# Low halves of the weights made by GpSimd in 256-column instructions instead of one instruction a tile

## Chip, cores and metric

The kernel runs on one core of a Trainium2 chip. The metric is the device time of one execution in microseconds (us); a run's time is the slowest core's, and there is one. Engines are named as the profile names them: PE is TensorE (PEld its weight loads), DVE is VectorE, ACT is ScalarE, POOL is GpSimd, SP is SyncE, which issues the DMAs.

## What is computed

The reference is a whole transformer block followed by a second block, on one sequence of 1024 tokens of width 1024, in float32. What matters here is that nearly all of it is matrix products of activations with weights:

```python
def first_block(x, ...):
        h = rmsnorm(x, norm_mix[l])
        proj = h @ w_in[l]
        y_a = retention(...) @ w_ret_o[l]
        y_b = nsa(...) @ w_nsa_o[l]
        merged = jax.nn.sigmoid(ga) * y_a + jax.nn.sigmoid(gb) * y_b
        x = x + merged @ w_out[l]
        x = x + conv_ffn(rmsnorm(x, norm_ffn[l]), w_up[l], conv_w[l], conv_b[l], w_down[l])
def second_block(x, c, ...):
        ada = c_act @ w_ada[l] + b_ada[l]
        proj = h @ w_in[l]
        mix = jnp.concatenate([y_rwkv, y_s5], axis=-1) @ w_out[l]
        ffn = (jax.nn.silu(h @ ffn_w_gate[l]) * (h @ ffn_w_up[l])) @ ffn_w_down[l]
```

`retention`, `nsa` (block-sparse attention), `rwkv7_time_mix` and `s5_mix` are sequence mixers between these products.

## The kernel before

**Products in split precision.** PE multiplies in the faster float32r format, so every operand is kept as two parts, a high part (rounded to float32r) and a low part (what the rounding left). A product of a weight tile and an activation is three sums: high x high, high x low, low x high. `mm3` (L216) issues them for one output tile of 128 x 512: first the 16 products with the weight's high part, then the 8 with its low part (for eight slices of 128 of the contraction, `kt` = 8). `mm3t` (L225) does it with weights as the moving operand.

**Loading a weight.** `wload` (L182) makes one tile of 128 output columns. SP loads the raw float32 weight into `wraw`, a tile of 128 partitions by up to eight slices of 128 columns (1024 columns; 512 or 640 where the contraction is shorter) at L197. ACT rounds it into `whi` (L199). POOL subtracts to make `wlo` (L200). `whi` and `wlo` have two buffers each, `wraw` two and, once there is room, a third that every third load goes to. So a buffer of `wlo` is free again when PE has done the low products of the tile before last, and a buffer of `wraw` when POOL has read it. `wload2` (L203) makes a pair of tiles side by side (`w2hi`, `w2lo`) with one subtraction for each of them at L213. `proj` (L234) calls `wload`, then `mm3` for one or two halves of the tokens, and evacuates each.

```python
        nc.scalar.activation(hi[:, :kt], raw[:, :kt], AF.Copy)
        nc.gpsimd.tensor_sub(lo[:, :kt], raw[:, :kt], hi[:, :kt].bitcast(F32))
```

**What else runs beside it.** DVE works on activations in SBUF: in the first feed-forward network `conv_gelu` (L1583) makes a convolution of width three from `at` into `ct` (L1596 to L1598), ACT applies the gelu (L1599), DVE multiplies by the second projection (L1616), ACT rounds to `ah` (L1617), and POOL makes `al` (L1618); `ah` and `al` are the operands of `down` (L1622). In `z_proj` (L1757) DVE makes the token shift in `ct` (L1772 to L1775). `s5_prep` (L995) builds tables of complex powers with long runs of DVE products of two SBUF tiles (L1072 to L1077), between the steps of that feed-forward network. `ada` (L1930) multiplies 96 weight tiles of 128 x 512 with a vector on DVE (L1943) beside the retention. `square_sum` (L255) adds squares at L263.

**What sets the order.** Each engine runs its instructions in a fixed order. It is chosen when the program is built, by a scheduler that goes by its own timing model, within the program's data dependencies and some extra edges (`side_by_side`, `hold`) that set the recurrent mixers and the feed-forward products side by side on PE. So a change of one instruction's size can move others. Dependencies are tracked by the region of a tile: a product waits for the writer of the slice that it reads.

Of the kernel before, what the change touches and what calls it, by code (L numbers as in the profile page):

```python
# [9 lines left out]
F32 = mybir.dt.float32  # L10
# [108 lines left out]
class Ctx:  # L119
# [62 lines left out]
    def wload(self, srcs, kt=KT, pool=None):  # L182

        nc = self.nc
        W = pool or self.W
        m = KT if pool is None else kt
        nb = 2 if pool is None else 1
        self.n_w += 1

        third = pool is None and self.WX is not None and self.n_w % 3 == 0  # L190
        raw = (self.WX if third else W).tile([128, m, 128], F32, name="wraw", bufs=1 if third else nb)
        hi = W.tile([128, m, 128], F32R, name="whi", bufs=nb)
        lo = W.tile([128, m, 128], F32R, name="wlo", bufs=nb)
        c = 0
        for src in srcs if isinstance(srcs, (list, tuple)) else [srcs]:
            n = src.shape[1]
            nc.sync.dma_start(raw[:, :kt, c:c + n], src.rearrange("(k p) n -> p k n", p=128))  # L197
            c += n
        nc.scalar.activation(hi[:, :kt], raw[:, :kt], AF.Copy)  # L199
        nc.gpsimd.tensor_sub(lo[:, :kt], raw[:, :kt], hi[:, :kt].bitcast(F32))  # L200
        return hi, lo

    def wload2(self, srcs, pool, kt=KT):  # L203

        nc = self.nc
        hi = pool.tile([128, kt, 256], F32R, name="w2hi")
        lo = pool.tile([128, kt, 256], F32R, name="w2lo")
        for e, src in enumerate(srcs):
            raw = self.W.tile([128, KT, 128], F32, name="wraw", bufs=2)
            nc.sync.dma_start(raw[:, :kt], src.rearrange("(k p) n -> p k n", p=128))  # L210
            sl = slice(e * 128, (e + 1) * 128)
            nc.scalar.activation(hi[:, :, sl], raw[:, :kt], AF.Copy)
            nc.gpsimd.tensor_sub(lo[:, :, sl], raw[:, :kt], hi[:, :, sl].bitcast(F32))  # L213
        return hi, lo

    def mm3(self, ps, w, a, t, kt=KT, late=False):  # L216
# [1797 lines left out]
```

## Time and profile before

| | |
|---|---|
| three runs | 3491.17 us median, 3486.78 to 3498.57 |
| the profiled execution | 3491.11 us, of which 3489.1 us are the span of its instructions |
| PE busy | 3350.0 us, 96% of the span |
| DVE busy | 1716.8 us, 49% |
| POOL busy | 1442.0 us, 41% |
| ACT busy | 1336.8 us, 38% |
| mean granted clock of PE | 0.982 of full speed |
| DMA | 371 MB, mean 106 GB/s |

An engine's busy time is the union of its instructions' spans, and an instruction that is held up while it runs counts as busy: a long mean duration can be work or a wait inside the instruction. Waits ahead of an instruction are idle time, put down to what ended them. PE's instructions overlap, and 48 products of 512 columns in a row take 48 equal steps, so the idle time of PE and the stretches at a lower clock are what can be gained there.

### The profile page before, as it was taken

What the parts mean: (1) busy time and instruction counts of PE and PEld (TensorE: products, weight loads), DVE (VectorE), ACT (ScalarE), POOL (GpSimd) and SP (SyncE); (2) the same over time, 40 slices, a digit from 0 to 9 for tenths busy, and PEclk for the clock granted to TensorE, in tenths of its full rate; (3) what the DMA queues carried; (4) which work ended last, traced back from release to release, by engine and by line L of the source; (5) the groups of instructions that cost most, each with busy time, mean ns of one, the idle gap of its engine ahead of it and who ended that gap; (6) DMA issues with size and microseconds to landing.
All of it is one profiled execution on the core that took longest, in us unless ns stands there. A gap on an engine that the chain in (4) does not pass through costs nothing. (4 is left out here: it accounts for less than half of the span.)

```text
span 3489.1 us, 49441 instructions
## 1 busy us (share of the span) xinstructions
PE 3350.0 (96%) x19080; PEld 2716.6 (78%) x19080; DVE 1716.8 (49%) x3313; ACT 1336.8 (38%) x2175; POOL 1442.0 (41%) x1081
## 2 busy tenths in 40 slices
PE   7999999998999998999989999999899999999998
PEld 6988788887788777887876777768777777778887
DVE  4456556555533774355674554564734344351112
ACT  4245346422334422243234444433353433342223
POOL 2333333210144444554554444325554443355544
PEclk9999999999999999999999999989999999999999
DMA  4211111455534434334533122234442221363332
GB/s 148 67 61 52 57 63 46 135 187 169 189 124 139 124 101 144 94 118 133 179 108 114 54 73 69 61 108 147 145 120 67 70 67 55 94 197 97 91 94 93
DMA packets 519813, 371.02 MB, mean 106 GB/s; under 512 B 31724, under 2 KB 455834, under 8 KB 518810
## 3 DMA queue, kind: packets, MB, share of 16 engines
q1 hardware_dynamic: 519578, 367.86, 34.3%
q8 instruction: 151, 2.47, 0.3%
q14 instruction: 84, 0.69, 0.1%
HBM read 313.44 MB, written 54.03 MB: 105 GB/s over the span
## 5 line engine op out<-in xcount | busy, mean ns | idle before, releaser
L200 POOL TENSOR_TENSOR wlo<-wraw,whi 128x1024 fp32r<-128x1024 f32 (+2 forms) x460 | 940.6, 2049 | 1290.7 <-PE mm L223 503.5
L199 ACT ACTIVATE whi<-wraw 128x1024 fp32r<-128x1024 f32 (+2 forms) x460 | 417.4, 909 | 703.7 <-PE mm L223 342.0
L223 PE MATMUL mm<-fh,whi 128*128 128x512 f32 x976 | 401.4, 413 | 10.0 <-ACT whi L199 4.9
L223 PE MATMUL mm<-fl,whi 128*128 128x512 f32 x976 | 393.2, 404 | 6.2 <-DVE fl L334 6.1
L223 PE MATMUL mm<-fh,wlo 128*128 128x512 f32 x976 | 270.2, 404 | 0.0
L223 PE MATMUL mm<-hh,whi 128*128 128x512 f32 x640 | 260.4, 407 | 5.4 <-DVE kc L252 3.7
L223 PE MATMUL mm<-hl,whi 128*128 128x512 f32 x640 | 260.9, 408 | 0.0
L223 PEld LDWEIGHTS mm<-fh,whi 128*128 128x128 f32 x976 | 185.9, 191 | 57.2 <-issue 6.5
L223 PEld LDWEIGHTS mm<-fl,whi 128*128 128x128 f32 x976 | 185.7, 191 | 47.0 <-DVE fl L334 9.3
L223 PE MATMUL b<-fh,whi 128*128 128x512 f32 x544 | 213.7, 393 | 1.2 <-ACT whi L199 0.7
L223 PE MATMUL b<-fl,whi 128*128 128x512 f32 x544 | 213.4, 392 | 0.0
L223 PEld LDWEIGHTS mm<-fh,wlo 128*128 128x128 f32 x976 | 179.0, 190 | 40.3 <-issue 3.6
L223 PE MATMUL mm<-ah,whi 128*128 128x512 f32 x429 | 177.1, 415 | 15.0 <-ACT ah L1617 9.3
L223 PE MATMUL mm<-hh,wlo 128*128 128x512 f32 x640 | 178.0, 400 | 0.0
L223 PE MATMUL mm<-al,whi 128*128 128x512 f32 x429 | 174.8, 408 | 0.0
L223 PEld LDWEIGHTS mm<-hh,whi 128*128 128x128 f32 x640 | 122.2, 191 | 27.9 <-issue 5.5
L223 PE MATMUL b<-fh,wlo 128*128 128x512 f32 x544 | 135.0, 390 | 6.3 <-POOL wlo L200 6.3
L223 PEld LDWEIGHTS mm<-hl,whi 128*128 128x128 f32 x640 | 122.1, 191 | 20.9
L223 PEld LDWEIGHTS mm<-hh,wlo 128*128 128x128 f32 x640 | 117.0, 189 | 21.5
L223 PE MATMUL mm<-ah,wlo 128*128 128x512 f32 x429 | 128.2, 407 | 0.3 <-POOL wlo L200 0.3
L588 ACT ACTIVATE s<-s,amn 128x640 f32<-128x640 f32 (+7 forms) x128 | 94.0, 735 | 80.3 <-DVE amn L584 74.3
L223 PEld LDWEIGHTS b<-fh,wlo 128*128 128x128 f32 x544 | 102.1, 188 | 28.3 <-POOL wlo L200 7.1
(601 smaller groups left out, 7117.5 us busy)
## 6 DMA issues: line engine op xcount, KB each, us to landing
wraw<-in_w_up SPq DMA_DIRECT2D x88, 512.0 KB
wraw<-in_w_in SPq DMA_DIRECT2D x84, 512.0 KB
ada_w<-in_w_ada SPq DMA_DIRECT2D x96, 256.0 KB
wraw<-in_ffn_w_gate SPq DMA_DIRECT2D x44, 512.0 KB
wraw<-in_ffn_w_up SPq DMA_DIRECT2D x44, 512.0 KB
wraw<-in_w_out SPq DMA_DIRECT2D x32, 512.0 KB
d_gab<-st SPq DMA_DIRECT2D x56, 256.0 KB
wraw<-in_w_down SPq DMA_DIRECT2D x48, 256.0 KB
```

Of the source, the lines that this page charges most:

```text
L199: nc.scalar.activation(hi[:, :kt], raw[:, :kt], AF.Copy)
L200: nc.gpsimd.tensor_sub(lo[:, :kt], raw[:, :kt], hi[:, :kt].bitcast(F32))
L223: self.nc.tensor.matmul(ps, w[x][:, k], a[y][k][:, t * 512:(t + 1) * 512], start=i == 0, stop=i == 3 * kt - 1)
L588: nc.scalar.activation(sb[r][:, :n], sb[r][:, :n], AF.Exp, bias=init, scale=-1.0, accum_out=st[:, 0, r:r + 1])
```

## The change

`wload` and `wload2` issue the subtraction for two slices (256 columns) at a time: four instructions for a tile of 1024 columns, two for 512, and for 640 two of 256 and one of 128. What is computed stays the same.

```diff
@@ wload
         nc.scalar.activation(hi[:, :kt], raw[:, :kt], AF.Copy)
-        nc.gpsimd.tensor_sub(lo[:, :kt], raw[:, :kt], hi[:, :kt].bitcast(F32))
+        for k in range(0, kt, 2):
+            sl = slice(k, min(k + 2, kt))
+            nc.gpsimd.tensor_sub(lo[:, sl], raw[:, sl], hi[:, sl].bitcast(F32))
         return hi, lo
@@ wload2
             nc.scalar.activation(hi[:, :, sl], raw[:, :kt], AF.Copy)
-            nc.gpsimd.tensor_sub(lo[:, :, sl], raw[:, :kt], hi[:, :, sl].bitcast(F32))
+            for k in range(0, kt, 2):
+                nc.gpsimd.tensor_sub(lo[:, k:k + 2, sl], raw[:, k:k + 2], hi[:, k:k + 2, sl].bitcast(F32))
```

Lines behind the first edit move by two, behind the second by three (L200 becomes L202, L223 becomes L226).

The change moves instructions. On PE, the low products of the first weight tile (`hh` is the activation's high part, `wlo` the weight's low part; Pool_49 is the semaphore that POOL raises) stood so before:

```order
L223 MATMUL mm<-hh_86,wlo 128x512 [waits Pool_49]
L223 MATMUL mm<-hh_87,wlo 128x512
L223 MATMUL mm<-hh_88,wlo 128x512
L223 MATMUL mm<-hh_89,wlo 128x512
L223 MATMUL mm<-hh_90,wlo 128x512
L223 MATMUL mm<-hh_91,wlo 128x512
L223 MATMUL mm<-hh_92,wlo 128x512
L223 MATMUL mm<-hh_93,wlo 128x512
```

and with the change:

```order
L226 MATMUL mm<-hh_86,wlo 128x512 [waits Pool_49]
L226 MATMUL mm<-hh_87,wlo 128x512
L226 MATMUL mm<-hh_88,wlo 128x512 [waits Pool_49]
L226 MATMUL mm<-hh_89,wlo 128x512
L226 MATMUL mm<-hh_90,wlo 128x512 [waits Pool_49]
L226 MATMUL mm<-hh_91,wlo 128x512
L226 MATMUL mm<-hh_92,wlo 128x512 [waits Pool_49]
L226 MATMUL mm<-hh_93,wlo 128x512
```

Each pair of products waits for its own piece; the pieces of a tile stand next to each other on POOL.

On PE in the first feed-forward network (its products at 1427 us of the trace of before; `b` and `mm` are the sums of two different weight tiles, `fh` and `fl` the activation), before:

```order
L223 MATMUL mm<-fh_9790,whi 128x512
L223 MATMUL mm<-fl_9798,whi 128x512
L223 MATMUL mm<-fh_9791,whi 128x512
L223 MATMUL mm<-fl_9799,whi 128x512
L223 MATMUL mm<-fh_9792,whi 128x512
L223 MATMUL mm<-fl_9800,whi 128x512
L223 MATMUL b_12781<-fh_9788,wlo 128x512
L223 MATMUL b_12781<-fh_9789,wlo 128x512
L223 MATMUL b_12781<-fh_9790,wlo 128x512
L223 MATMUL b_12781<-fh_9791,wlo 128x512
```

and with the change:

```order
L226 MATMUL mm<-fh_9965,whi 128x512
L226 MATMUL b_13132<-fh_9964,wlo 128x512
L226 MATMUL b_13132<-fh_9965,wlo 128x512
L226 MATMUL mm<-fl_9973,whi 128x512
L226 MATMUL b_13132<-fh_9966,wlo 128x512
L226 MATMUL b_13132<-fh_9967,wlo 128x512
L226 MATMUL mm<-fh_9966,whi 128x512
L226 MATMUL b_13132<-fh_9968,wlo 128x512
L226 MATMUL b_13132<-fh_9969,wlo 128x512
L226 MATMUL mm<-fl_9974,whi 128x512
```

The low products of the earlier tile moved ahead of high products of the later one, a pair at a time. Such a place occurs a few times; about one PE instruction in eleven has another place in the order than before, most of them in the attention and the retention, where two streams of products stand side by side.

## Rows read from the trace of the kernel before

**Rows 1.** The page's first part: busy time, share of the span, instructions.
```profile
span 3489.1 us, 49441 instructions
...
PE 3350.0 (96%) x19080; PEld 2716.6 (78%) x19080; DVE 1716.8 (49%) x3313; ACT 1336.8 (38%) x2175; POOL 1442.0 (41%) x1081
```

**Rows 2.** PE's waits: for whom, us in total, times, longest.
```profile
PE mm L223 <- ACT ah L1617: 9.3, 1, 9.3
...
PE b L223 <- POOL wlo L200: 6.3, 2, 3.4
...
PE mm L231 <- DVE ct L1616: 4.3, 1, 4.3
```

**Rows 3.** Busy time in four stretches: PE, PEld, DVE, ACT, POOL; then granted clock, DMA.
```profile
650.00:900.00 250.00, 229.09 (x1404) 203.27 (x1403) 142.76 (x275) 66.42 (x107) 34.06 (x14) 0.98 0.54 168
1100.00:1350.00 250.00, 231.03 (x1145) 190.01 (x1144) 164.00 (x367) 84.51 (x123) 110.54 (x73) 0.97 0.42 126
1550.00:1800.00 250.00, 230.46 (x1157) 195.83 (x1156) 165.35 (x179) 80.05 (x114) 131.39 (x102) 0.95 0.47 147
...
2400.00:2600.00 200.00, 188.56 (x944) 159.25 (x942) 104.31 (x115) 76.45 (x104) 104.69 (x67) 0.96 0.41 126
```

**Rows 4.** POOL's groups by shape: busy us, mean ns, idle before and its releasers.
```profile
L200 POOL TENSOR_TENSOR wlo<-wraw,whi 128x1024 fp32r<-128x1024 f32 x284 | 689.2, 2429 | 882.6 <-PE mm L223 351.6 <-ACT whi L199 270.5 <-issue 94.7
L200 POOL TENSOR_TENSOR wlo<-wraw,whi 128x512 fp32r<-128x512 f32 x112 | 146.4, 1313 | 289.2 <-PE mm L223 125.7 <-ACT whi L199 83.9 <-PE b L223 52.2
L200 POOL TENSOR_TENSOR wlo<-wraw,whi 128x640 fp32r<-128x640 f32 x64 | 105.2, 1649 | 119.0 <-ACT whi L199 36.0 <-PE b L223 35.7 <-PE mm L223 26.2
...
L593 POOL TENSOR_SCALAR s<-s,ast 128x640 f32<-128x640 f32 x40 | 31.4, 805 | 33.9 <-DVE ast L591 21.7 <-ACT pth L605 12.2
...
L1440 POOL TENSOR_TENSOR TT<-TT,bon 128x256 f32<-128x256 f32 x16 | 12.2, 761 | 22.7 <-ACT TT L1437 22.7
```

**Rows 5.** DVE's groups by shape, columns as in rows 4.
```profile
L263 DVE TENSOR_TENSOR nacc<-nacc,nsq 128x512 f32<-128x512 f32 x76 | 71.2, 942 | 28.3 <-ACT nsq L262 27.7
L1596 DVE TENSOR_SCALAR ct<-at,pc_b 128x512 f32<-128x512 f32 x44 | 68.3, 1554 | 90.7 <-ACT at L1592 90.6
L1772 DVE TENSOR_TENSOR ct<-at 128x512 f32<-128x512 f32 x28 | 52.7, 1882 | 44.9 <-ACT at L1768 44.9
...
L1616 DVE TENSOR_TENSOR ct<-ct,mm 128x512 f32<-128x512 f32 x53 | 36.3, 684 | 90.2 <-PE mm L223 83.2 <-ACT ct L1610 3.7 <-ACT ct L1599 2.9
```

**Rows 6.** Timeline, 1191 to 1197.5 us: start, duration, instruction, idle before it.
```profile
1191.44 2.79 POOL L1618 TENSOR_TENSOR al<-ct,ah 128x512 fp32r<-128x512 f32 x1 [3.53 <-ACT ah L1617]
...
1192.41 0.69 DVE L1077 TENSOR_TENSOR s_ba<-s_m,s_m 128x512 f32<-128x512 f32 x1
...
1193.01 1.50 DVE L1596 TENSOR_SCALAR ct<-at,pc_b 128x512 f32<-128x512 f32 x1
...
1194.19 2.52 POOL L200 TENSOR_TENSOR wlo<-wraw,whi 128x1024 fp32r<-128x1024 f32 x1
...
1194.55 2.71 DVE L1597 SCALAR_TENSOR_TENSOR ct<-at,pc_b,ct 128x512 f32<-128x512 f32 x1
```

**Rows 7.** Timeline, 1609.4 to 1615.6 us.
```profile
1610.07 2.53 POOL L200 TENSOR_TENSOR wlo<-wraw,whi 128x1024 fp32r<-128x1024 f32 x1
...
1610.43 2.72 DVE L1597 SCALAR_TENSOR_TENSOR ct<-at,pc_b,ct 128x512 f32<-128x512 f32 x1
...
1615.43 0.58 PE L231 MATMUL mm<-w2hi,mh 128*128 128x256 f32 x1 [4.29 <-DVE ct L1616]
```

**Rows 8.** Timeline of POOL, 254 to 258 us.
```profile
254.06 3.14 POOL L593 TENSOR_SCALAR s<-s,ast 128x640 f32<-128x640 f32 x4 [4.67 <-ACT pth L605]
```

**Rows 9.** The chain that ended last, in order of time: start, us, what.
```profile
3061.43 10.88 PE b L223 x48
```

**Rows 10.** SP's waits: for whom, us in total, times, longest.
```profile
SPq L197 <- POOL wlo L200: 1521.1, 349, 12.5
```

**Rows 11.** ACT's waits, columns as in rows 10.
```profile
ACT whi L199 <- PE mm L223: 342.0, 149, 6.5
```

## The prediction

> **What bounds the kernel now.** I read the page's busy times first. PE is busy for 3350.0 of 3489.1 us [rows 1], so 139.1 us of its idle time, and what it loses at a lower clock, are all that can be won while its work stays the same. The windows show where that lies: four stretches of 950 us together hold 20.9 + 19.0 + 19.5 + 11.4 = 70.8 us of PE's idle time, half of all, and their granted clock of 0.95 to 0.98 (most of the time at 2.4 GHz, some of it at 1.2) takes another 5.0 + 7.5 + 12.5 + 8.0 = 33.0 us (length times the share not granted) [rows 3]. The other half of the idle time is spread thin over 2540 us, and I expect nothing from it.
>
> PE's own waits come next. It waits for POOL's `wlo` hardly at all: the larger of two groups has 6.3 us in two waits [rows 2]. The changed instruction is therefore no bound in itself. PE waits for DVE and for ACT behind DVE, as for `ct` and for `ah`, where one wait alone is 9.3 us [rows 2].
>
> So why is DVE late in those stretches? The groups by shape tell. L1616, a product of 512 columns with one operand in PSUM, takes 684 ns. L1596, L1772 and L263 work on as many columns with all operands in SBUF, and take 1554, 1882 and 942 ns on average [rows 5]. At the price of L1616 these three alone lose 870 x 44 + 1198 x 28 + 258 x 76 ns = 38 + 34 + 20 = 91 us inside the instruction. The timeline shows to whom: L1597 begins at 1194.55 while POOL has been at L200 since 1194.19; L200 ends at 1196.71, and L1597 at 1197.26, 0.55 us later [rows 6]. The same pair stands at 1610.07 and 1610.43: L1597 takes 2.72 us, some 2.0 more than undisturbed, and the chain from it through gelu and L1616 ends PE's wait of 4.29 us at 1615.43 [rows 7]. DVE and POOL shut each other out for whole instructions, and L200 with its 2.4 us is the longest that POOL does often.
>
> **The change, part by part.**
>
> *Price of a piece.* The step from 512 to 1024 columns is 2429 - 1313 = 1116 ns, 2.18 ns a column, so 256 columns take 1313 - 558 = 755 ns, which L1440 with its 761 ns for 256 columns of two operands bears out, and 128 columns 476 [rows 4]. A tile of 1024 becomes 4 x 755 = 3020 ns, 591 more; one of 512 becomes 1510, 197 more; one of 640 becomes 1986, 337 more. Over 284, 112 and 64 tiles that is 168 + 22 + 22 = 212 us, with `wload2`'s 16 tiles some 220, in about 1140 more instructions; POOL goes from 1442 to about 1660 us, 48% of the span. Back to back, four instructions of L593 take 3.14 us where one is 805 ns on average, so the step is about 778 and the overlap 28 ns [rows 4, 8]. The Trainium skill, Perfetto Trace Analysis, section GPSIMD Engine Instruction, holds POOL's reported spans to be unreliable and wants the spacing of consecutive starts instead. By it the sum would be 1140 x 28 ns = 32 us smaller, by the durations it stays at 220. I take the durations; neither is on PE's path.
>
> *What covers it.* `wlo` has two buffers, so POOL may start when PE has finished the tile before last. With 10.88 us for 48 products [rows 9], 227 ns each, PE then has the 24 products of one tile and the 16 high ones of the next to do: 9.1 us until the first piece is needed. 3.0 us fit three times. If the cover were gone, every tile would cost up to 0.59 us, 460 of them 270 us at the very most; I charge nothing for undisturbed tiles.
>
> *Queues behind it.* `wraw` is freed 0.59 us later, and SP, which waits for that in 349 loads for 1521.1 us together [rows 10], issues the next load and all behind it so much later. But ACT, which needs the load, waits for PE to free `whi` (342.0 us in 149 waits in the largest group [rows 11]), so loads land in time. Bounds: nothing, to 0.59 us where a load is the last to come; I take nothing. On POOL itself `al`, the attention's scales and the mixers' products stand behind L200 and come up to 0.59 us later.
>
> *Gain for PE waiting on `wlo`.* The first piece is there after 755 instead of 2429 ns. At 755 ns for a pair and 454 for its products, the last product ends at 3.02 + 0.45 = 3.47 us instead of 2.43 + 1.82 = 4.25. That is 0.8 us in each of a few waits: -2 us. The three more semaphore waits per tile on PE I cost at nothing where the piece is ready; no row shows one alone. Bounds: nothing, or 0.1 us (half a product) for each of some 1000, 100 us, if they held up the pipeline; the nearest row is the 48 products in 10.88 us [rows 9], two tiles with one such wait each, at an even pace, so I take nothing.
>
> *Gain for DVE.* A wait behind L200 can last one piece, 755 ns, instead of one tile, 2429. Of the 91 us above that leaves about 28 (91 x 755 / 2429), if DVE gets its turn between two pieces. It does between two whole instructions: L1596 waits for `al`, which ends at 1194.23, and is done 0.28 us later, while L200, which starts at 1194.19, takes 2.52 us, 0.09 more than its mean: DVE got in ahead of it [rows 4, 6].
>
> *How much of it reaches PE.* At 1615 us L1597 would give back 1.2 us (2.0 less a whole piece) to 2.0 us of a wait of 4.29, 28 to 46% [rows 7]. I take a third of the idle time in the four stretches: -24 us. The lower clock comes behind such idle stretches, and I let it follow them: a third of 33.0, -11 us. Bounds: nothing, since a second engine may end the same wait; and two thirds of both, -69.
>
> *Lateness of POOL.* Where DVE runs through products of two SBUF tiles without a break, POOL cannot get in: `al` was issued at 1191.44, and took 2.79 us, 1.5 more than two operands of 512 columns take on POOL, until that run ended with L1077 [rows 4, 6]. Now a tile can lose its turn at four borders. For this, and for the moved order, I charge +10 us; bounds: nothing, and the rival below.
>
> **Sum.** Against the profiled execution of 3491.1 us, which is the median of the three runs as well: -24 - 11 - 2 + 10 = -27, so 3464 us. A measurement of this kernel can tell about 0.3%, 10 us, from no change.
>
> **Rivals.**
>
> *DVE's gain stays hidden.* PE's order is fixed, and behind a wait that shrinks the next late operand takes over: DMA for the `ada` weights in the first stretch, DVE's own length in the others (164 and 165 of 250 us busy [rows 3]). For it: DVE's busy time includes work that must be done anyway. Against: the waits inside instructions are plain in the rows. Then only small change remains, about -5: 3486 us. Chance 0.17.
>
> *POOL starves, and `wlo` becomes the bound.* In the second and third stretch DVE and POOL together are busy for 275 and 297 of 250 us [rows 3], so they contend almost always. A piece that loses 1.5 us at each of four borders makes a tile of 3.0 + 6.0 = 9.0 us, just the 9.1 that PE leaves. Beyond that point each tile's lateness is PE's, and the moved order makes PE ask for it earlier. If ten tiles come 3 us late, that is +30, while the gain is halved to -14: about 3507 us, slower. Against it: POOL's mean over all tiles is 2429 ns, hardly disturbed [rows 4]; today DVE loses nearly every contest. The Trainium skill, SBUF — State Buffer, section Who interferes with whom, says that issue order decides who blocks, for the whole instruction; by it four issues are four chances to lose, which is this rival. Chance 0.12.
>
> *The turn is not handed over between pieces.* If POOL's pieces followed each other so closely that DVE never got in, a wait would grow from 2.43 to 3.02 us. On some 100 waits that is 59 us of DVE's time, a third of it PE's: +20, 3511 us. L1596 at 1193.01 speaks against it. Chance 0.06.
>
> The forecast, with gains from 10 us on, keeps 0.65. So faster 0.65, same 0.17, slower 0.18. The range takes in most of the bound of two thirds below and the lower part of the slower cases: 3428 to 3502.
>
> **What would show it.** Right: L1596, L1772 and L263 have means below 1.0, 1.2 and 0.8 us; the pieces take about 755 ns each and POOL is busy for some 1650 us; PE's idle time in the four stretches falls from 70.8 to under 50 us and their clock rises. Wrong: PE's waits for `wlo` grow from 6.3 to over 20 us (starving), or the DVE means stay (no handing over), or they fall while PE's idle time stays (hidden).

## The result and the profile after

The changed kernel takes 3457.44 us (median of four runs, 3450.65 to 3460.05), the kernel before, in the same set, 3490.74 (3486.78 to 3498.57). The ratio is 0.9898, with a 95% interval of 0.9884 to 0.9911: 33 us less, where 27 were forecast. The trace of the change is that of its quickest run, 3450.65 us, and the trace of before that of a middle one, so what the two traces differ by is some 7 us more than the medians do.

The first part of the page of the changed kernel answers to [rows 1]:

```profile
span 3448.9 us, 51023 instructions
...
PE 3344.0 (97%) x19080; PEld 2711.0 (79%) x19080; DVE 1587.6 (46%) x3313; ACT 1330.1 (39%) x2170; POOL 1701.5 (49%) x2221
```

PE's idle time, span less busy, fell from 139.1 to 104.9 us, and its mean granted clock rose from 0.982 to 0.984, which is 62.8 against 55.2 us lost (span times the share not granted). Together that is 41.8 us less; the span fell by 40.2. The groups by shape of the changed kernel, POOL's first, then DVE's, answer to [rows 4, 5] (busy us, mean ns, idle before and its releasers):

```profile
L202 POOL TENSOR_TENSOR wlo<-wraw,whi 128x256 fp32r<-128x256 f32 x1488 | 1169.3, 816 | 1129.4 <-ACT whi L199 586.3 <-issue 269.6 <-PE mm L226 88.6
```

```profile
L266 DVE TENSOR_TENSOR nacc<-nacc,nsq 128x512 f32<-128x512 f32 x76 | 64.3, 855 | 29.4 <-ACT nsq L265 29.1
...
L1599 DVE TENSOR_SCALAR ct<-at,pc_b 128x512 f32<-128x512 f32 x44 | 39.0, 887 | 91.6 <-ACT at L1595 91.5
...
L1619 DVE TENSOR_TENSOR ct<-ct,mm 128x512 f32<-128x512 f32 x53 | 36.3, 684 | 95.0 <-PE mm L226 87.9 <-ACT ct L1613 3.7 <-ACT ct L1602 3.0
...
L1775 DVE TENSOR_TENSOR ct<-at 128x512 f32<-128x512 f32 x28 | 23.0, 823 | 67.0 <-ACT at L1771 67.0
```

The convolution product fell from 1554 to 887 ns, the token shift from 1882 to 823, the sum of squares from 942 to 855, while L1619, which reads PSUM, stayed at 684. The four stretches of [rows 3] now (PE, PEld, DVE, ACT, POOL; granted clock, DMA):

```profile
650.00:900.00 250.00, 244.20 (x1509) 217.88 (x1508) 140.57 (x296) 69.41 (x112) 52.57 (x62) 1.00 0.58 181
1100.00:1350.00 250.00, 234.30 (x1129) 190.13 (x1128) 163.14 (x370) 82.15 (x118) 144.23 (x194) 0.97 0.44 128
1550.00:1800.00 250.00, 240.09 (x1236) 203.86 (x1235) 137.92 (x182) 92.19 (x129) 173.50 (x222) 0.99 0.46 146
2400.00:2600.00 200.00, 186.64 (x995) 153.53 (x994) 95.24 (x126) 83.90 (x117) 128.66 (x152) 0.94 0.42 129
```

Idle time there is 5.8 + 15.7 + 9.9 + 13.4 = 44.8 us (70.8 before) and the clock takes 0 + 7.5 + 2.5 + 12.0 = 22.0 (33.0). The same times hold slightly later work than before, since the program runs ahead. The last stretch reads worse, 25.4 us lost against 19.4, because a stop at 2585 us and the beginning of a slow stretch behind it, both explained below, fall into it. PE's waits of the changed kernel that matter, with [rows 2]:

```profile
PE mm L226 <- ACT ah L1620: 8.9, 2, 8.6
...
PE b L1382 <- DVE T L1362: 4.1, 1, 4.1
...
PE b L226 <- POOL wlo L202: 3.6, 5, 1.9
...
PE mm L234 <- DVE ct L1619: 2.8, 1, 2.8
```

The wait for `wlo` has not grown. The 4.1 us for `T` is new in size, and will be explained below. Summed over the whole list, PE's waits that DVE ended fell from 85.8 to 53.8 us, while those that ACT ended (27.8 and 26.8), that POOL ended (8.3 and 6.7), and that the profile puts to issue (6.7 and 7.4) stayed nearly as they were. So nearly all of the idle time that went had been waiting for DVE.

### The profile page after: what moved, and what is told of

It reads as the page before. It is cut to its first block, busy times and chain, and to the rows that moved or that the text cites. A ratio compares the mean times of both kernels' runs of the same rounds, so it can differ in the third digit from the quotient of the medians.

```text
span 3448.9 us, 51023 instructions
## 1 busy us (share of the span) xinstructions
PE 3344.0 (97%) x19080; PEld 2711.0 (79%) x19080; DVE 1587.6 (46%) x3313; ACT 1330.1 (39%) x2170; POOL 1701.5 (49%) x2221
## 5 line engine op out<-in xcount | busy, mean ns | idle before, releaser
L202 POOL TENSOR_TENSOR wlo<-wraw,whi 128x256 fp32r<-128x256 f32 (+1 forms) x1552 | 1200.3, 804 | 1129.4 <-ACT whi L199 586.3
L226 PE MATMUL mm<-fh,whi 128*128 128x512 f32 x976 | 403.9, 416 | 7.5 <-ACT fh L336 4.4
L226 PE MATMUL mm<-fl,whi 128*128 128x512 f32 x976 | 395.3, 406 | 4.1 <-DVE fl L337 4.0
L226 PE MATMUL mm<-fh,wlo 128*128 128x512 f32 x976 | 272.4, 406 | 0.0
L226 PE MATMUL mm<-hh,whi 128*128 128x512 f32 x640 | 258.6, 404 | 3.8 <-DVE kc L255 2.8
L226 PE MATMUL mm<-hl,whi 128*128 128x512 f32 x640 | 258.8, 405 | 0.0
L226 PEld LDWEIGHTS mm<-fh,whi 128*128 128x128 f32 x976 | 186.8, 192 | 53.3 <-ACT fh L336 5.6
L226 PEld LDWEIGHTS mm<-fl,whi 128*128 128x128 f32 x976 | 187.2, 192 | 46.1 <-DVE fl L337 7.1
L226 PE MATMUL b<-fh,whi 128*128 128x512 f32 x544 | 212.4, 390 | 0.9 <-ACT whi L199 0.5
L226 PE MATMUL b<-fl,whi 128*128 128x512 f32 x544 | 211.9, 390 | 0.0
L226 PEld LDWEIGHTS mm<-fh,wlo 128*128 128x128 f32 x976 | 180.0, 191 | 39.8 <-issue 2.6
L226 PE MATMUL mm<-ah,whi 128*128 128x512 f32 x429 | 174.8, 410 | 11.8 <-ACT ah L1620 8.9
L226 PE MATMUL mm<-hh,wlo 128*128 128x512 f32 x640 | 178.4, 400 | 0.0
L226 PE MATMUL mm<-al,whi 128*128 128x512 f32 x429 | 172.7, 403 | 0.2 <-DVE al L1621 0.2
L226 PE MATMUL b<-fh,wlo 128*128 128x512 f32 x544 | 139.1, 392 | 3.6 <-POOL wlo L202 3.6
L226 PEld LDWEIGHTS mm<-hh,whi 128*128 128x128 f32 x640 | 121.1, 189 | 25.8 <-issue 3.2
L226 PEld LDWEIGHTS mm<-hl,whi 128*128 128x128 f32 x640 | 121.2, 189 | 20.8
L226 PEld LDWEIGHTS mm<-hh,wlo 128*128 128x128 f32 x640 | 117.0, 188 | 21.8
L226 PE MATMUL mm<-ah,wlo 128*128 128x512 f32 x429 | 128.8, 406 | 0.7 <-POOL wlo L202 0.7
L596 POOL TENSOR_SCALAR s<-s,ast 128x640 f32<-128x640 f32 (+7 forms) x128 | 88.4, 713 | 78.4 <-DVE ast L594 48.9
```

Of the source, the lines that this page charges most:

```text
L202: nc.gpsimd.tensor_sub(lo[:, sl], raw[:, sl], hi[:, sl].bitcast(F32))
L226: self.nc.tensor.matmul(ps, w[x][:, k], a[y][k][:, t * 512:(t + 1) * 512], start=i == 0, stop=i == 3 * kt - 1)
L596: nc.gpsimd.tensor_scalar(sb[r][:, :n], sb[r][:, :n], st[:, 2, r:r + 1], 1.0, op0=OP.mult, op1=OP.mult)
```

## Experiments

Three causes could give such a result. **A**: DVE waits for a piece instead of a tile. **B**: the moved order of instructions. **C**: PE can start the low products on the first piece.

**Sizes of a piece.** Steps of four and of one slice instead of two:

```diff
-        for k in range(0, kt, 2):
+        for k in range(0, kt, 4):
```

> Two pieces of 512 columns for a tile of 1024 instead of four of 256. Theory A (the gain is that DVE's two-tensor instructions wait for a piece instead of for a tile): the longest wait is half of a tile's, so part of the gain stays: 12 to 24 us below the kernel before (3467 to 3479 us), DVE's convolution product a mean between 1.05 and 1.3 us (1.55 us before, 0.89 us with 256 columns), POOL about 1530 us. Theory B (the gain is the changed order of the instructions): no relation to the size of the pieces, anything between 3450 and 3500 us. Theory C (the gain is that PE's low products start on the first piece of a tile): about half of the gain, as A, but with PE's waits for wlo in proportion and not with DVE's means.

Measured: 3460.75 us, ratio 0.9906 (0.9885 to 0.9928), 32 us below before; POOL 1546.0 us, as expected, and the convolution product at 1034 ns, just under what A gave. The gain is larger than A expected: half the cut gave all the gain.

> Eight pieces of 128 columns for a tile of 1024. By the 128-column instructions of the change (534 ns against 816 ns for 256) a tile costs POOL some 4.3 us instead of 3.3 us, POOL about 2090 us in all. Theory A: DVE's waits shrink again, the convolution product to 0.8 us or less, and the time lies 0 to 10 us below the change (3447 to 3457 us), if POOL keeps up. Rival (POOL becomes late): PE's waits for wlo go over 20 us and the time lies 10 us or more above the change. Theory B: no relation, 3450 to 3500 us.

Measured: 3467.84 us, ratio 0.9932 (0.9910 to 0.9954), 10 us slower than the change by the medians of two sets, whose intervals just touch (0.9911 is the upper end of the change). The convolution product is at 790 ns, POOL at 1965.1 us, less than the 2090 expected, and still PE's largest group of waits for `wlo` has 4.6 us in four. So DVE gained as A says, and POOL was not late as the rival has it; but the time did not follow DVE. Neither A nor the rival explains these 10 us, as far as they are real.

**Order of the low products.** In the change and in the kernel before, for `mm3t` alike:

```diff
-[(k, 1, 0) for k in range(kt)]
+[(k, 1, 0) for k in reversed(range(kt))]
```

> The change, but the low products of each tile run from the last slice to the first, so that the first low product waits for the last piece as it waited for the whole tile before. Theory A: the gain stays, 3450 to 3465 us, and DVE's convolution product stays near 0.89 us. Theory C (the early start on the first piece): the gain goes, 3480 us or more. Theory B: the order of PE's products is another one again, so the time moves by 10 us or more with DVE's means as in the change.

> The kernel before with whole tiles on POOL, only the low products run from the last slice to the first. Theories A and C: no change, 3484 to 3498 us, DVE's convolution product near 1.55 us. Theory B: how far an order of products alone moves the time: 10 us or more from the kernel before, in either direction.

Measured: with pieces 3473.85 us, ratio 0.9942 (0.9922 to 0.9962), with whole tiles 3495.62 us, 1.0011 (0.9998 to 1.0024). The second is no change. The first falls between A and C, and seemed to give C half of the gain. But the scheduler had made a new order for it, so cause and order were still mixed.

**The order held.** The next kernels take the order out of the scheduler's hands: a list of all instructions of each engine, in the order of one built kernel, is laid down as edges that fix the sequence and add no wait.

```diff
+def pin(tc):
+    ins = list(tc.nc.cur_bb.bb.instructions)
...
+    for steps in json.loads(zlib.decompress(base64.b85decode(ORDERED))):
+        at, last = 0, None
+        for s in steps:
+            at += s
+            if last is not None:
+                tc.add_manual_dep(ins[at], last.name, no_sync, reason="pinned")
+            last = ins[at]
...
-        g.fill(g.C, FIRST)
+        g.fill(g.C, FIRST); pin(tc)
```

> The pieces of 256 columns, with every engine's instructions held in the order of the kernel before (the pieces of a tile stand where the tile stood). What is left of the change is the shorter instruction on POOL and that a low product waits for its own piece only; no order is changed. Theory A (DVE's shorter waits carry the gain): most of the gain is here, 3452 to 3470 us, DVE's convolution product below 1.0 us. Theory B (the changed order carries it): 3483 us or more, DVE's means as in theory A.

> The counterpart: whole tiles on POOL, with every engine's instructions held in the order of the change. Theory A: the gain is gone, 3480 to 3500 us, DVE's convolution product at 1.4 us or more. Theory B: the gain is here, 3450 to 3468 us, though DVE's means are those of the kernel before.

Measured: pieces in the old order 3458.71 us, ratio 0.9916 (0.9896 to 0.9937), 32 us below before; whole tiles in the new order 3478.85 us, 0.9971 (0.9957 to 0.9984), 12 below. The convolution product is at 924 and 1480 ns. So the pieces alone carry as much as the whole change, with no instruction in another place: A holds. The order alone is worth 12 us, more than A allowed and less than B asked; its interval lies just below no change. The two do not add up (32 and 12 against 33, by the medians), so the new order seems also to lose something where pieces are made. Where it helps can be seen in the retention. First pieces in the old order, then whole tiles in the new:

```profile
650.00:900.00 250.00, 237.03 (x1431) 209.06 (x1430) 136.78 (x293) 67.92 (x108) 50.17 (x60) 0.97 0.55 170
```

```profile
650.00:900.00 250.00, 238.66 (x1480) 213.84 (x1479) 142.03 (x278) 70.40 (x114) 37.61 (x15) 0.98 0.57 176
```

PE is busy for 229.09 us there before [rows 3], 237.03 with the pieces alone, 238.66 with the order alone, and 244.20 with both. These are single traces, and the one of whole tiles in the new order is of its longest run, 3496.97 us: it shows where the order helps, not the 12 us.

**The early start.** In the kernel with pieces in the old order, POOL's loop runs backwards; nothing else moves.

```diff
-        for k in range(0, kt, 2):
+        for k in reversed(range(0, kt, 2)):
```

> As the pieces in the order of the kernel before, but POOL makes the pieces of a tile from the last slice to the first, so that the first low product, which needs slice 0, waits until all are made. No other instruction has another place. Theory C (early start on the first piece): 8 us or more slower than that kernel. Theory A: within 4 us of it.

Measured: 3459.06 us, ratio 0.9911 (0.9895 to 0.9927), 0.35 us from the kernel it is compared with. PE's waits for `wlo` and `w2lo` grew with it, from 7.1 to 13.4 us in the two traces, so the early start saves PE a few us of waiting; in the medians nothing of that shows. C falls as the cause of the gain. What the reversed low products lost before must then have come with the scheduler's new order; where was not traced.

**What the new order loses.** In the recurrent mixer (`unit_pair`) POOL makes `TT` in three instructions (L1359, L1361), DVE transposes it into `T` (L1362), PE multiplies `T` in products of 32 columns (L1382), and DVE and PE then take turns on it (L1383 to L1392). The timelines of the change show such a chain, at the start of the second half's mixer. POOL, then DVE, then PE (start, duration, instruction, idle before it):

```profile
2578.09 3.26 POOL L202 TENSOR_TENSOR wlo<-wraw,whi 128x256 fp32r<-128x256 f32 x4
2581.32 1.05 POOL L1526 TENSOR_TENSOR bp<-kk,PP 128x512 f32<-128x512 f32 x1
2582.34 2.82 POOL L202 TENSOR_TENSOR wlo<-wraw,whi 128x256 fp32r<-128x256 f32 x4
2585.13 1.25 POOL L1621 TENSOR_TENSOR al<-ct,ah 128x512 fp32r<-128x512 f32 x1
2586.35 1.51 POOL L1359 TENSOR_TENSOR TT<-G,c_m2t 64x256 f32<-64x256 f32 x2
2587.93 0.72 POOL L1361 TENSOR_TENSOR TT<-TT,c_i 128x256 f32<-128x256 f32 x1
```

```profile
2578.17 1.22 DVE L1521 SCALAR_TENSOR_TENSOR kk<-kk,PI 128x512 f32<-128x512 f32 x1 [4.47 <-POOL kk L1520]
...
2581.08 1.29 DVE L1348 TENSOR_TENSOR G<-b,c_maskg 128x512 f32<-128x512 f32 x2 [0.73 <-PE b L1345]
2588.69 0.45 DVE L1362 STREAM_TRANSPOSE T<-TT 128x256 f32<-128x256 f32 x1 [6.32 <-POOL TT L1361]
```

```profile
2584.80 0.39 PE L226 MATMUL mm<-fl,whi 128*128 128x512 f32 x1
2589.28 1.07 PE L1382 MATMUL b<-T,G 64*64 64x32 f32 x16 [4.10 <-DVE T L1362]
2590.28 0.79 PE L226 MATMUL mm<-fh,whi 128*128 128x512 f32 x1
```

`G`, the input, is ready at 2582.37, but POOL's fixed order puts a tile and an `al` ahead of `TT`, which starts 4.0 us later; PE stands still for 4.1 us. Two kernels ask whether this matters. The first takes 512 columns from the second feed-forward network on, a size with which PE waited only 1.2 us for `T`, in an order of the scheduler's own; the second leaves the change as it is, pins its own order, and moves only those three instructions on POOL.

```diff
+    g.n = 4
     f20 = F.steps(2, 0)
...
-        for k in range(0, kt, 2):
+        for k in range(0, kt, self.n):
```

> Pieces of 256 columns up to the second feed-forward network, of 512 from there on. In the change PE stands still for 4.1 us at 2584.8 us of its trace, waiting for a chain POOL to DVE to PE behind eight pieces of two tiles, and then runs 37.5 us at the lower clock. If the pieces of 256 columns made that chain late: the stretch at the lower clock goes, and the time lies 8 to 18 us below the change, 3440 to 3450 us. If it hangs on something else: 3453 to 3465 us with the same stretch.

Measured: 3444.55 us, ratio 0.9879 (0.9851 to 0.9906), inside the range for a chain that was late, although one of its six runs took 3473.63 us; PE waits 1.2 us there, and the clock is 0.99 from 2560 to 2680 us.

The order of POOL in the second kernel, against that of the change:

```
 L202 TENSOR_TENSOR wlo<-wraw,whi 128x256 x4
 L1526 TENSOR_TENSOR bp<-kk,PP 128x512
-L202 TENSOR_TENSOR wlo<-wraw,whi 128x256 x4
-L1621 TENSOR_TENSOR al_25430<-ct,ah_25429 128x512
 L1359 TENSOR_TENSOR TT_22583<-G,c_m2t 64x256 x2
 L1361 TENSOR_TENSOR TT_22583<-TT_22583,c_i_22463 128x256
+L202 TENSOR_TENSOR wlo<-wraw,whi 128x256 x4
+L1621 TENSOR_TENSOR al_25430<-ct,ah_25429 128x512
```

> The change with its own order on every engine, but at one place: POOL's three instructions of the chain before 2584.8 us (two TT products, one TT sum, 2.2 us together) stand ahead of the four pieces and the al that ran just before them (4.0 us). If that order costs the 4.1 us stop and the stop the 37.5 us at the lower clock: PE's wait for T there falls below 1.5 us, the stretch at the lower clock goes, and the time lies 12 to 20 us below the change, 3437 to 3446 us. If the stretch at the lower clock comes from the small products that PE runs there and not from the stop: only the 2 to 4 us of the stop, 3453 to 3456 us, and the stretch stays.

Measured: 3441.51 us (3439.67 to 3448.22), ratio 0.9856 (0.9834 to 0.9877), the lowest median of all kernels here. PE's wait for `T` is gone from its list, and the stretch behind it runs at full clock. The windows of the change, then of this kernel:

```profile
2560.00:2680.00 120.00, 115.08 (x806) 84.23 (x805) 43.67 (x102) 39.54 (x65) 56.33 (x73) 0.84 0.20 61
2590.00:2627.00 37.00, 37.00 (x240) 25.37 (x238) 9.42 (x20) 7.89 (x10) 11.16 (x12) 0.53 0.07 19
```

```profile
2560.00:2680.00 120.00, 118.69 (x903) 87.14 (x903) 49.07 (x110) 50.92 (x82) 67.07 (x89) 1.00 0.28 84
2590.00:2627.00 37.00, 36.87 (x333) 25.93 (x332) 13.96 (x30) 17.55 (x30) 23.66 (x29) 1.00 0.20 58
```

In the same 37 us PE does 240 products in the one and 333 in the other, "busy" throughout in both. By the share of the clock that was not granted (0.53 is nearly all at 1.2 GHz) that is an estimated 17 us. PE's order is the same in both kernels, so the time can also be taken between the same two products: the last ahead of the stop, and one behind the slow stretch. In the change they start at 2584.80 (above) and

```profile
2637.18 0.39 PE L226 MATMUL mm<-fl,whi 128*128 128x512 f32 x1
```

and with the moved chain at

```profile
2593.47 0.40 PE L226 MATMUL mm<-fl,whi 128*128 128x512 f32 x1
...
2626.62 0.39 PE L226 MATMUL mm<-fl,whi 128*128 128x512 f32 x1
```

So the same work takes 52.4 us in the one and 33.1 in the other, 19 us from one place in POOL's order of some 2200 instructions; by the medians of the next set it is 15.

**The last set.** The kernel with two sizes was also tried with `al` in halves of 256 columns, and it and the change were run again on the same chip as the kernel just described.

```diff
-            (nc.vector if last else nc.gpsimd).tensor_sub(lo, c, hi.bitcast(F32))
+            for h in [slice(0, 512)] if last else [slice(0, 256), slice(256, 512)]:
+                (nc.vector if last else nc.gpsimd).tensor_sub(lo[:, h], c[:, h], hi[:, h].bitcast(F32))
```

> The kernel with 256 columns up to the second feed-forward network and 512 from there, and POOL's al (512 columns, 1.25 us) in two instructions of 256 columns as well. Theory A, if it holds for any instruction of POOL on two tensors: DVE loses some 8 us less to al, which gives 1 to 6 us, 3437 to 3445 us. If al stands at the chains' ends, where its own length counts: 1 to 5 us slower than without, 3445 to 3450 us.

> The change itself, beside the others of this set on the same chip: 3450 to 3462 us.

> The kernel with 256 columns up to the second feed-forward network and 512 from there, once more on the same chip as the change: 3438 to 3450 us, 8 to 18 us below the change.

Measured: 3455.58 us, ratio 0.9889 (0.9863 to 0.9916) with `al` in halves, above both of its ranges; 3456.17, 0.9890 (0.9864 to 0.9916) for the change again; 3450.28, 0.9875 (0.9851 to 0.9899) for the two sizes again, just above its range. The halves say nothing about `al`: the scheduler's order changed with them, and the mixer's stretch from 2560 to 2680 us runs at 0.83 again. The two sizes are 6 to 13 us below the change by medians, and the intervals overlap: a probable gain, not a shown one. That the moved chain beats the change by 15 us rests on the medians of one set, whose intervals overlap at the edge (0.9864 and 0.9877), and on the traces above. The six runs of the change again go from 3443.57 to 3465.34 us, with mean granted clocks between 0.988 and 0.980, and the trace is that of the longest; its two shortest runs come as low as the moved chain's (3439.67 to 3448.22). Whether those two had the slow stretch no trace shows.

**The same products in every trace.** In all the traces PE's 13,938th product of 19,080 is the last ahead of this chain, and the 14,250th stands behind it. The time between their starts, and what each trace has gained by the first of them on the trace of before (us):

| trace | between the two | gained before them |
|---|---|---|
| before | 34.0 | |
| the change, twice | 52.4, 54.6 | 55.3, 44.2 |
| the change with the chain moved | 33.1 | 46.6 |
| two sizes, twice | 34.2, 34.2 | 44.5, 39.8 |
| two sizes, `al` in halves | 50.6 | 44.7 |
| 128 columns | 54.3 | 45.0 |
| 512 columns | 34.2 | 28.5 |
| pieces, low products reversed | 52.9 | 34.1 |
| whole tiles, low products reversed | 34.0 | -6.9 |
| pieces in the old order, forwards and backwards | 34.5, 34.5 | 36.6, 33.4 |
| whole tiles in the new order | 48.9 | 9.2 |

So this stretch costs some 34 us in eight traces and 15 to 21 more in the other six. It also hides what the size of a piece is worth: up to there 512 columns have gained less than 128 or 256 in orders close to the change's, and then lose nothing, while the change gives back 18 to 21 us. Each figure is of one trace.

## Why the prediction was right, point by point

- **Bound and mechanism: right, and shown.** DVE held up behind POOL's long instructions was the cause; the pieces in the old order gave 32 us without any other change. The pair of instructions most like each other, DVE's L1521 of the change (above) and the same instruction with whole tiles in the new order, POOL ahead of DVE:

```profile
2619.90 2.38 POOL L200 TENSOR_TENSOR wlo<-wraw,whi 128x1024 fp32r<-128x1024 f32 x1
```

```profile
2619.98 2.86 DVE L1518 SCALAR_TENSOR_TENSOR kk<-kk,PI 128x512 f32<-128x512 f32 x1 [1.87 <-POOL kk L1517]
```

  Both start 0.08 us behind POOL; beside a whole tile it takes 2.86 us and ends behind the tile, beside four pieces 1.22 us and ends while POOL still has 2 us to go. So the turn is handed over between pieces, and that rival falls. At the wait that the forecast worked through, L1597 (now L1600, at 1582.26) takes 1.10 us instead of 2.72, and PE waits 2.84 us instead of 4.29 [rows 7]: 34% less, where 28 to 46% were forecast. The Trainium skill, SBUF — State Buffer, section Who interferes with whom, says that a DVE instruction with two SBUF inputs contends with a GpSimd instruction that reads SBUF, for a port pair that is an exclusive lock, and that issue order decides who blocks. Both pairs of rows agree, with 2.86 and 1.22 us, and show what follows: the unit of waiting is the instruction, not the tile.

- **DVE's loss, forecast to shrink from 91 to 28 us:** at the price of L1619 it is now 203 x 44 + 139 x 28 + 171 x 76 ns = 8.9 + 3.9 + 13.0 = 25.8 us. The bars for L1596 and L1772 were met; L263's, 0.8 us, was set too low: even with pieces of 128 columns it takes 831 ns. L1597, whose 2.7 us the forecast read from two places of the timeline, was no typical case: its mean was 983 ns before, and is 1026 now.

- **Idle time, -24, and clock, -11, in the four stretches:** -26.0 and -11.0, in the trace of the quickest run. "I expect nothing" from the rest was wrong by a little: all idle time fell by 34.2 us. And the clock gave back outside the stretches 3.4 of the 11.0 us that it won in them, since the mixer's slow stretch lies mostly there. The sum came out near in part by luck, because these two miss in opposite directions. Nor was the gain a third of each stretch: the first gave back 20.1 us of idle time and clock, the second 3.3, and the wait of 9.3 us for `ah` [rows 2], which the forecast named as one behind DVE, is still 8.6 us.

- **Price of a piece, 755 ns:** undersized. The mean is 816, POOL rose by 259.5 us and not by 220. Four pieces that nobody disturbs take 2.82 us, 705 each; beside L1521 and what follows it on DVE, four take 3.26 (timeline above). The rest of the mean I put down to DVE, which now gets its turns; it was not measured apart. None of it reached PE as a wait for `wlo`: -2 us was forecast, and the largest group went from 6.3 to 3.6. With 128 columns POOL was busy for 263.6 us more still, and that wait stayed at 4.6. The cover of 9.1 us a tile held, and the rival of the starving POOL falls in the form in which it was put.

- **Queues and moved order, charged at +10 us:** a true cost, undersized and put in the wrong place. I looked for it in tiles that lose their turn at borders. It sits in one chain of the mixer behind a tile and an `al` in POOL's order, and cost 18 to 21 us in the two traces of the change against that of before. Against it stands what the order gains elsewhere, 12 us net with whole tiles, much of it in the retention, which I had not forecast. The two nearly cancel: 32 us with the pieces in the old order, 33 in the new.

- **The hidden gain:** falls. Of the 65 us that DVE won inside those three instructions (91 less 25.8), PE got back a part: its idle time fell by 34.2 us. With the old order, too, its waits for DVE fell, from 85.8 to 59.1 us.

## To carry to other kernels

Where two engines shut each other out for whole instructions, cut the longer instruction of the one off the critical path: the other's wait shrinks to a piece, at the price of the pieces' fixed cost, and only as long as the cut engine has slack. A change of one instruction's size can reorder a scheduled program, and that alone moved this one by 12 us, and by 15 to 21 at one place; to learn what an edit is worth, hold every engine's order and change the instruction alone. After that, look in the new order for short chains that stand behind long filler work on a helper engine.

## What the runs showed of the hardware that was not expected

In the same part of the mixer PE ran for 37 us at 0.53 of the clock after a stop of 4.1 us, and at 1.00 without it, although PE was busy to 100% in both. The length of that stop does not decide alone: with whole tiles in the new order PE stopped there for 1.1 us only, and the stretch still ran low, while with pieces in the old order it stopped for 1.5 us and kept its clock. With `al` in halves it stopped for 1.3 us and the clock fell, with the two sizes for 1.2 us and it did not. The windows, first of whole tiles in the new order (the same work lies 40 us later), then of pieces in the old order:

```profile
2600.00:2720.00 120.00, 116.43 (x794) 85.05 (x793) 49.15 (x100) 42.56 (x68) 50.70 (x40) 0.84 0.21 63
```

```profile
2560.00:2680.00 120.00, 115.07 (x866) 85.00 (x864) 45.99 (x102) 52.87 (x79) 65.63 (x85) 1.00 0.29 87
```

What tips the clock at the entry to that stretch stays open. It is known only that in the trace with the chain moved forward the slow stretch is gone. Since pieces of 128 columns, the reversed low products and `al` in halves met it, and 512 columns and the old order did not, it made a part of the scatter between these kernels. It cannot be why 128 columns and the reversed low products with pieces lie above the change, which met it as well.

Nor was it expected that the size of a piece would matter so little: 512 columns gave 32 us, 256 gave 33. The traces above suggest why: ahead of the slow stretch 256 columns had gained more, and lost it there. Each ran in an order of its own, so what the last cut alone is worth was not separated.
